# Slots of one SBUF ring padded from 8,224 to 8,448 bytes

## The chip, the cores and the metric

The kernel runs on one core of a Trainium2 chip. The metric is the device time in microseconds; the kernel before was timed three times, with a median of 2720.2 us (2720.13 to 2723.26). One more execution was taken with the hardware profiler; all rows below are from that one. Engines: PE is TensorE's matmul, PEld its weight load, DVE VectorE, ACT ScalarE, POOL GpSimd, SP the engine that issues the DMAs.

## The reference

One encoder block over 2,048 positions of width 1,024, in float32:

```python
mod = silu(c) @ w_ada + b_ada                       # shift, scale, gate, twice
h = rms_norm(x, norm1_g) * (1 + scale1) + shift1
q, k, v, xr, gr = split(h @ w_in)                   # 5 x 512 columns
attn = dilated_mixture_attention(q, k, v, positions)    # 8 heads, 3 dilations
rec = bidirectional_rg_lru(xr, gr, ...)             # conv, gates, two scans, gelu gate
mixed = concat([rms_norm(attn, attn_out_g), rms_norm(rec, lru_out_g)])
x = x + gate1 * (mixed @ w_out)
h2 = rms_norm(x, norm2_g) * (1 + scale2) + shift2
x = x + gate2 * (square(relu(h2 @ w_ff1)) @ w_ff2)  # 1024 -> 4096 -> 1024
return rms_norm(x, final_g)
```

## The kernel before

**Matmuls.** Every large product is made of float32r matmuls in which both operands are split into a rounded high half and a remainder (`halves`, `wsplit`): high x high, high x low, low x high, three matmuls for one. Nearly all go through `mm` (L89). The second argument of `mm` is the operand that is loaded as weights (128 columns of 4 bytes, so 512 bytes of each partition); the third is the one that moves through the array (mostly 512 columns, so 2,048 bytes of each partition). In a row of the trace such a matmul reads `pmm<-moving,weights`: `pmm`, `pg` and `ptr` are the three rings of PSUM banks.

**Stages, in order of time.** The six modulation vectors (`ada`) and the projections by `w_in` (to about 660 us; weights in `wh`, activations in `hT`; the recurrence runs beside them), attention (to about 1,217 us), `w_out` (`wout_tile`, to about 1,360 us), the first feed-forward matrix (FFN1, to about 2,050 us) and the second (FFN2, to the end). Both feed-forward products use a seven-product scheme over 2 x 2 blocks (`LEFT`, `RIGHT`). In FFN1 a step of the loop over `steps1` is 12 matmuls; its weights, split by `w1_prep`, lie in three tiles of tag `L8` (`new_slots`), and what moves is `hT`, `wh` or, for one product, two further `L8` tiles. In FFN2 a step of `steps2` is 24 matmuls; its weights are the hidden blocks, which `prep2` writes into a new `L8` tile at each step (ACT rounds at L1508, POOL subtracts at L1510), and what moves is `wf`. There are 7 x 16 = 112 such steps; the first 96 are those of the products that come before the last one in `ORD2`. During the last product DVE also finishes the rows of the output (`finals`).

**Rings.** A tile is taken from a ring of slots by its tag (`sbt`, with the number of slots in `BUFS`): `L8` has 6 slots, `st` 6, `hT` 8, `wh` 4, `r4` 4, `t2` 8, `bc` 2, `wf` 4, `xr` 4, `C` 16. A ring's slot is as large as the largest tile of its tag. Most tiles of `L8` have 8,192 bytes in each partition; four, the `xrn` tiles, have `S + 8` = 2,056 numbers, 8,224 bytes. So the six `L8` slots lie 8,224 bytes apart. `L8` and `st` come first in their memory; all other rings lie behind `L8`. In the built program the slots begin at these places:

| ring | start of its slots, bytes past a multiple of 256 | past a multiple of 512 |
|---|---|---|
| `L8`, slots 0 to 5 | 0, 32, 64, 96, 128, 160 | 0, 32, 64, 96, 128, 160 |
| `st`, `t2`, `bc`, `hT`, `r4`, `wh`, `wf`, `xr`, `w2`, `C`, `xt`, `row` | 192 | 192 |

The other slots' sizes are multiples of 512. The weights of a matmul begin a multiple of 512 bytes into their slot in all of the 512-column matmuls spoken of below. FFN1's three weight tiles lie in slots 0, 3 and 5; FFN2's step goes through all six slots in turn (in the trace's stretch from 2184.68 us: slots 1, 5, 4, 3, 0, 2).

```python
xrn = [sbt("L8", (P, S + 8)) for j in range(4)]                       # L470
w, (hi, lo) = wslot[(s + 4) % 6], bks[m]                              # FFN1, a step
for l, r in ((w[:, 0, ks], hi[:, k]), (w[:, 0, ks], lo[:, k]), (w[:, 1, ks], hi[:, k])):
    mm(pt, l, r, n == 0, n == 11)
mm(pts[i], h[:, 0, ts], w[:, 0], p == 0, False)                       # FFN2, 8 tiles of a step
mm(pts[i], h[:, 0, ts], w[:, 1], False, False)
mm(pts[i], h[:, 1, ts], w[:, 0], False, p == NP - 1)
```

The order of the work is that of the program: every engine takes its instructions as they are written, and all DMAs are issued by SP.

Of the kernel before, what the change touches and what calls it, by code (L numbers as in the profile page):

```python
# [17 lines left out]
P = 128  # L18
S = 2048
# [37 lines left out]
def block_kernel(ctx: ExitStack, tc, x, vecs, pos, w_ada, b_ada, fg, w_in, lwa, lwx, w_out, w1, w2, cst, out):  # L57
# [13 lines left out]
    def sbt(tag, shape, dt=F32):  # L71
        cnt[0] += 1
        return (sx if tag in ("L8", "st") else sb[0]).tile(list(shape), dt, tag=tag, name=f"{tag}_{cnt[0]}", bufs=BUFS[tag])
# [393 lines left out]
    for t in xs:  # L467
        norm_x(t)
    SY.dma_start(Done, onr)
    xrn = [sbt("L8", (P, S + 8)) for j in range(4)]  # L470
    for j in range(4):
        G.memset(xrn[j][:, 0:2], 0.0)
        G.memset(xrn[j][:, S + 2:S + 8], 0.0)
# [1174 lines left out]
```

## Time and profile before

| what | value |
|---|---|
| median of three runs | 2720.2 us (2720.13 to 2723.26) |
| the profiled execution: its own time, its span | 2720.57 us, 2718.7 us |
| mean granted TensorE clock | 0.949 |
| PE, PEld busy | 94%, 76% of the span |
| DVE, POOL, ACT busy | 61%, 44%, 40% |
| DMA engines busy (main queue) | 55.4% |

A busy PE in this table is not a PE at its peak: matmuls overlap, and their ends are modelled. What one matmul takes from the next is read from their starts: so many in so many microseconds.

### The profile page before, as it was taken

Reading aid. Unit: us, or ns where it says so; the run is one execution under the profiler, and the core shown is the slowest. Engines: PE = TensorE matmul, PEld = TensorE weight load, DVE = VectorE, ACT = ScalarE, POOL = GpSimd, SP = SyncE. Lnnn points to the kernel's source line nnn. Section 1 sums busy time; section 2 is a strip of 40 time slices with the busy share of each in tenths; the row PEclk is TensorE's granted clock in tenths of the full one; section 3 lists DMA queues with packets and bytes.
Section 4 is the critical chain, followed back from the end, with each engine's and each line's share of the span. In section 5 each row is a group of like instructions: output and inputs, shape, how many; then the busy total and the mean of one; then the engine's idle time right before and its main releaser. Section 6 shows DMA issues by size and latency. Waiting matters only on the chain.

```text
span 2718.7 us, 32852 instructions
## 1 busy us (share of the span) xinstructions
PE 2542.2 (94%) x11321; PEld 2075.0 (76%) x11321; DVE 1656.9 (61%) x2963; ACT 1093.5 (40%) x1701; POOL 1200.8 (44%) x914
## 2 busy tenths in 40 slices
PE   4998988999999999999879999899998999999996
PEld 3776767778888888887757877688886888888885
DVE  6588777974444444436767657977774224312688
ACT  2243675571122222222455445655553323232223
POOL 2343444642012211131357667766556445544544
PEclk9998989998898888899989999999998999999998
DMA  6765356566544455547766666644437465536554
GB/s 266 266 225 186 96 178 211 203 163 159 122 109 118 117 132 140 125 141 235 243 202 214 204 195 209 209 152 155 140 129 276 164 209 187 170 121 210 191 201 176
DMA packets 267491, 486.01 MB, mean 179 GB/s; under 512 B 88874, under 2 KB 122406, under 8 KB 259754
## 3 DMA queue, kind: packets, MB, share of 16 engines
q1 hardware_dynamic: 267324, 483.92, 55.4%
q8 instruction: 89, 1.46, 0.2%
q14 instruction: 78, 0.64, 0.1%
HBM read 330.45 MB, written 153.19 MB: 178 GB/s over the span
## 4 chain that ended last, share of the span: by engine, by line
PE 36%; POOL 6%; DVE 5%; DMA 5%; issue 3%; ACT 1%; SPq 0%; POOLq 0%; DVEq 0%; ACTq 0%
PE pmm L89 15%; PE pg L89 13%; PE ptr L89 8%; POOL st L1218 3%; DMA st<-Dh 3%; POOL ry L301 1%; DVE L L1223 1%; POOL t L1380 1%; DMA Dhc<-st 1%; POOL L L1510 0%; DVE C L1545 0%; DVE C L1549 0%; DVE L L1200 0%; POOL L L1381 0%; DMA r<-in_w 0%
## 5 line engine op out<-in xcount | busy, mean ns | idle before, releaser
L1510 POOL TENSOR_TENSOR L<-xr,L 128x512 fp32r<-128x512 f32 x224 | 317.5, 1438 | 285.9 <-ACT L L1508 278.7
L89 PE MATMUL pmm<-hT,wh 128*128 128x512 f32 x1536 | 376.1, 401 | 5.9 <-POOL hT L341 3.3
L89 PEld LDWEIGHTS pmm<-hT,wh 128*128 128x128 f32 x1536 | 293.6, 193 | 78.3 <-POOL hT L341 7.7
L89 PE MATMUL pmm<-wf,L 128*128 128x512 f32 x1008 | 292.4, 398 | 17.8 <-ACT L L1508 12.8
L89 PE MATMUL pg<-wf,L 128*128 128x512 f32 x1008 | 290.0, 396 | 0.0
L858 DVE CUSTOM_DVE_ANT_0 junk<-ptr,mb 128x256 bf16<-128x256 f32 (+2 forms) x384 | 140.1, 365 | 174.3 <-PE ptr L89 157.3
L89 PEld LDWEIGHTS pmm<-wf,L 128*128 128x128 f32 x1008 | 190.5, 189 | 65.2 <-ACT L L1508 13.2
L912 ACT ACTIVATE t<-pmm 128x512 f32<-128x512 f32 x160 | 94.8, 596 | 353.5 <-PE pmm L89 352.3
L1223 DVE TENSOR_TENSOR L<-st,L 128x512 fp32r<-128x512 f32 x167 | 191.4, 1151 | 63.3 <-ACT L L1222 62.0
L89 PEld LDWEIGHTS pg<-wf,L 128*128 128x128 f32 x1008 | 190.7, 189 | 45.2
L257 POOL TENSOR_TENSOR wh<-r,wh 128x512 fp32r<-128x512 f32 x88 | 139.8, 1610 | 173.5 <-DVE wh L95 106.1
L301 POOL TENSOR_TENSOR ry<-rv,mhalf 128x1 f32<-128x1 f32 x80 | 51.5, 645 | 350.4 <-DVE rv L299 341.3
L89 PE MATMUL ptr<-wf,L 128*128 128x512 f32 x672 | 193.9, 397 | 0.0
L1218 POOL TENSOR_TENSOR st<-r,r 128x512 f32<-128x512 f32 x96 | 135.9, 1423 | 109.3 <-DVE L L1223 94.7
L89 PE MATMUL pmm<-hT,hT 66*128 66x256 f32 (+5 forms) x672 | 177.1, 399 | 0.0
L1223 DVE TENSOR_TENSOR wf<-st,wf 128x512 fp32r<-128x512 f32 x80 | 59.8, 747 | 190.6 <-ACT wf L1222 190.6
L1222 ACT ACTIVATE L<-st 128x512 fp32r<-128x512 f32 x168 | 105.5, 628 | 163.6 <-POOL st L1218 84.9
L89 PE MATMUL ptr<-hT,hT 128*128 128x256 f32 (+5 forms) x672 | 163.6, 390 | 4.1 <-DVE mc L858 4.0
L1222 ACT ACTIVATE wf<-st 128x512 fp32r<-128x512 f32 x80 | 50.4, 631 | 281.7 <-PE pg L89 216.5
L89 PE MATMUL pg<-t,L 128*66 128x192 f32 (+2 forms) x756 | 159.0, 348 | 1.8 <-POOL L L1051 1.8
L89 PE MATMUL pmm<-hT,L 128*128 128x512 f32 x576 | 149.7, 408 | 10.0 <-ACT L L1222 7.1
L89 PEld LDWEIGHTS pmm<-hT,hT 128*128 128x128 f32 (+1 forms) x672 | 148.8, 278 | 9.1 <-issue 2.6
(326 smaller groups left out, 5276.3 us busy)
## 6 DMA issues: line engine op xcount, KB each, us to landing
xr<-Dhx SPq DMA_DIRECT2D x112, 512.0 KB
w<-in_w SPq DMA_DIRECT2D x192, 256.0 KB
r<-in_w SPq DMA_DIRECT2D x64, 512.0 KB
Dhx<-t SPq DMA_DIRECT2D x128, 256.0 KB
L<-in_w_ada SPq DMA_DIRECT2D x24, 1024.0 KB
r<-in_w_in SPq DMA_DIRECT2D x40, 512.0 KB
st<-Dh SPq DMA_DIRECT2D x72, 256.0 KB
r<-in_x SPq DMA_DIRECT2D x26, 512.0 KB
```

What stands on the lines that cost most here:

```text
L89: T.matmul(o, l, r, start=st, stop=sp, skip_group_check=True)
L257: G.tensor_tensor(w[:, 1, cs], raw[:, cs], f(w[:, 0, cs]), ALU.subtract)
L301: G.tensor_tensor(y, v_, mhalf[:, 0:1], ALU.pow)
L858: V.tensor_tensor_reduce(junk[:, 0:nk], p_[:, e, 0:nk], mb1[:, off:off + nk], 1.0, -3e38, ALU.add, ALU.max, mc[:, idx:idx + 1])
L912: A.activation(pf, pS, AF.Exp)
L1218: eng.tensor_tensor(o, a, b, ALU.add if sign > 0 else ALU.subtract)
L1222: A.activation(hi, raw, AF.Copy)
L1223: lo_eng.tensor_tensor(lo, raw, f(hi), ALU.subtract)
L1380: G.tensor_tensor(x6, x6, h, ALU.subtract)
L1510: G.tensor_tensor(h[:, 1, e], r_[:, e], f(h[:, 0, e]), ALU.subtract)
```

## The change

```diff
@@ -467,7 +467,7 @@
     for t in xs:
         norm_x(t)
     SY.dma_start(Done, onr)
-    xrn = [sbt("L8", (P, S + 8)) for j in range(4)]
+    xrn = [sbt("L8", (P, S + 64))[:, 0:S + 8] for j in range(4)]
     for j in range(4):
         G.memset(xrn[j][:, 0:2], 0.0)
         G.memset(xrn[j][:, S + 2:S + 8], 0.0)
```

The four `xrn` tiles are taken with 2,112 numbers and used as before with 2,056. The ring's slots become 8,448 bytes, and everything behind `L8` moves up by 6 x 224 = 1,344 bytes. Every engine has the same instructions in the same order with the same waits; the places in DRAM are the same. What differs is where operands lie in SBUF:

| ring | bytes past a multiple of 256, after | past a multiple of 512, after |
|---|---|---|
| `L8`, slots 0 to 5 | 0, 0, 0, 0, 0, 0 | 0, 256, 0, 256, 0, 256 |
| the others of the table above | 0 | 0 |

## Rows read from the trace of the kernel before

**Rows 1.** The page's first part: busy time, share, instructions of each engine.

```profile
PE 2542.2 (94%) x11321; PEld 2075.0 (76%) x11321; DVE 1656.9 (61%) x2963; ACT 1093.5 (40%) x1701; POOL 1200.8 (44%) x914
```

**Rows 2.** The page's fourth part: chain that ended last, by engine.

```profile
PE 36%; POOL 6%; DVE 5%; DMA 5%; issue 3%; ACT 1%; SPq 0%; POOLq 0%; DVEq 0%; ACTq 0%
```

**Rows 3.** Two windows: us, busy of each engine (instructions), clock, DMA share, GB/s.

```profile
2080.00:2600.00 520.00, 520.00 (x2239) 420.53 (x2238) 185.61 (x236) 163.01 (x214) 266.63 (x193) 1.00 0.54 187
1760.00:2040.00 280.00, 280.00 (x1204) 225.77 (x1203) 211.79 (x245) 161.31 (x273) 171.59 (x114) 1.00 0.41 146
```

**Rows 4.** The chain of waits from 1,599 us: start, length, what.

```profile
1599.93 5.43 DMA st<-Dh
...
1645.46 2.60 PE ptr L89 x10
...
1703.96 0.72 PE ptr L89 x3
...
1757.48 3.75 PE pg L89 x12
...
2032.37 2.80 PE pg L89 x12
...
2046.37 2.81 PE pmm L89 x12
...
2597.02 0.71 PE pg L89 x3
...
2599.11 0.60 DVE C L1532
```

**Rows 5.** PE timeline, moving and weights both at 192; last row: weights in `L8`.

```profile
95.67 20.11 PE L89 MATMUL pmm<-hT,wh 128*128 128x512 f32 x88
...
1217.85 11.15 PE L89 MATMUL pmm<-wh,r 128*128 128x512 f32 x48
...
1229.21 11.39 PE L89 MATMUL pmm<-wh,L 128*128 128x512 f32 x48
```

**Rows 6.** PE timeline in FFN2: the first row of seven successive steps.

```profile
2184.68 0.85 PE L89 MATMUL pmm<-wf,L 128*128 128x512 f32 x3
...
2190.29 0.86 PE L89 MATMUL pmm<-wf,L 128*128 128x512 f32 x3
...
2195.89 0.85 PE L89 MATMUL pmm<-wf,L 128*128 128x512 f32 x3
...
2201.39 0.86 PE L89 MATMUL pmm<-wf,L 128*128 128x512 f32 x3
...
2206.98 0.86 PE L89 MATMUL pmm<-wf,L 128*128 128x512 f32 x3
...
2212.58 0.87 PE L89 MATMUL pmm<-wf,L 128*128 128x512 f32 x3
...
2218.16 0.85 PE L89 MATMUL pmm<-wf,L 128*128 128x512 f32 x3
```

**Rows 7.** PE timeline in the recurrence: moving in `L8`, weights in `bc`.

```profile
287.07 1.56 PE L89 MATMUL pg<-L,bc 128*128 128x512 f32 x6
288.47 5.62 PE L89 MATMUL pmm<-hT,wh 128*128 128x512 f32 x24
```

**Rows 8.** Groups of 512-column matmuls with weights outside `L8`.

```profile
L89 PE MATMUL pmm<-hT,wh 128*128 128x512 f32 x1536 | 376.1, 401 | 5.9 <-POOL hT L341 3.3 <-DVE hT L340 1.1 <-DVE hT L341 1.0
L89 PE MATMUL pmm<-hT,r 128*128 128x512 f32 x384 | 100.6, 415 | 2.2 <-DVE L L1200 2.2
L89 PE MATMUL pmm<-wh,hT 128*128 128x512 f32 x384 | 96.0, 405 | 6.8 <-DVE st L411 6.8
```

**Rows 9.** DMA queue, 6.5-9, 9-11.5, 100.3-102.8 us: packets, MB, share of 16 engines.

```profile
q1 hardware_dynamic: 273, 1.05, 102.6%
...
q1 hardware_dynamic: 269, 1.04, 102.6%
...
q1 hardware_dynamic: 245, 0.95, 93.1%
```

## The prediction

> **What bounds the kernel now.** I read the busy time first: PE is at it for 94% of the span and no other engine for more than 61% [rows 1]. The average says little, so the next view is the chain of waits. Of its shares, PE has by far the largest, POOL, DVE and DMA 5 to 6% each [rows 2]. In order of time the chain has three kinds of stretch [rows 4]. Up to 1645 us, in the first part of FFN1, it runs through loads of `st` from `Dh`, POOL sums and evictions: PE is fed late there, and a faster PE would wait longer. From 1645.46 to 1704.68 us and from 1757.48 to 2049.18 us it is PE alone, one group of 12 matmuls behind the other. FFN2 is PE alone too, until its last product begins at about 2597 us and DVE's work on the output rows takes over. The two windows show the same from the other side: PE is busy for all of 520 and all of 280 us at granted clock 1.00, while DVE, ACT and POOL leave 24% and more free [rows 3].
>
> **What a matmul costs there, and on what that depends.** The change adds, removes and moves no instruction. It can act only through the places of operands in SBUF, so I looked for rows in which the same operation has operands in different places, and counted from start to start.
>
> Weights and moving operand both 192 bytes past a multiple of 256: 88 projections in a row span 20.11 us. A single one is modelled as 401 ns long on average [rows 8], overlapping the next, so from the first start to the last it is (20.11 - 0.40) us / 87 = 226.6 ns from one to the next [rows 5].
>
> Weights in `L8`, moving operand at 192: in `wout_tile`, the same lines with the weights in `r4` take (11.15 - 0.40) us / 47 = 228.7 ns, and 11 us later with the weights in `L8` (11.39 - 0.40) us / 47 = 233.8 ns [rows 5]. In FFN2, step after step of 24 matmuls with the same code and only another slot, the differences of the starts give 5.61, 5.60, 5.50, 5.59, 5.60, 5.58 us for slots 1, 5, 4, 3, 0, 2 [rows 6]: 233.8, 233.3, 229.2, 232.9, 233.3, 232.5 ns, on average 33.48 us / 144 = 232.5 ns. In FFN1, 2.80 us / 12 = 233.3 ns [rows 4].
>
> Moving operand in `L8`, weights in `bc` at 192: (288.47 - 287.07) us / 6 = 233.3 ns [rows 7].
>
> So a 512-column matmul costs 226.6 ns (228.7 in the shorter row) where both operands have the same remainder by 256 (and here by 512), and 229 to 234 ns where they differ, whichever of the two lies in `L8`. Slot 4, with its 229.2 ns, is only 64 bytes off. I read this as a cost of the difference of the two places. After the change that difference is 0 by 256 everywhere, and by 512 in slots 0, 2 and 4; in slots 1, 3 and 5 it is 256. No 512-column matmul of this trace has a difference of 256. Its cost is bounded by the rows from 226.6 ns (nothing lost) to 233.8 ns (the dearest row at full clock with weights in `L8`). I take 226.6, since every row fits a pattern that repeats every 256 bytes, but one that repeats every 512 fits nearly as well; both ends stay in the range.
>
> A rule speaks against any effect. The Trainium skill ("SBUF — State Buffer", section "Who interferes with whom") gives TensorE two independent SBUF read ports, one for the moving operand and one for the weights, and says that TensorE never waits on anyone. By that the sum would be 0 and the time 2720.6 us. The trace differs: 5.50 against 5.61 us for the same step, by slot alone [rows 6].
>
> **The sum.** It is made against the profiled execution, 2720.57 us (span 2718.7), 0.4 us above the median of 2720.2.
> - FFN2 up to the last product: 96 steps x 24 = 2,304 matmuls x (232.5 - 226.6 = 5.9 ns) = 13.6 us. All on the path: the chain is PE to 2597 us, and what follows on DVE starts from PE's evictions [rows 4].
> - FFN1 from 1757.48 to 2049.18 us: 291.7 / 0.2333 = 1,250 matmuls x 6.7 ns (233.3 - 226.6) = 8.4 us, on the path.
> - FFN1 from 1645.46 to 1704.68 us: 254 x 6.7 ns = 1.7 us, on the path; the feeders' stretch behind it starts from a PE row.
> - FFN1 otherwise: of its 224 steps x 12 = 2,688 matmuls 1,184 are left, most of them before 1645 us. They get shorter too, but the chain is the loads' and POOL's there; I count nothing. If the feeders were bound to PE after all it would be 1,184 x 6.7 ns = 7.9 us.
> - The two `w_out` tiles from `L8`: 48 x 7.2 ns = 0.3 us. The recurrence: 192 matmuls (4 column blocks, 2 x 2 gates, 4 stretches, 3 each) like those of rows 7 x 6.7 ns = 1.3 us; whether they are on the path the chain does not show, I take half, 0.6.
> - The last 16 steps of FFN2: DVE's chain; nothing.
> - VectorE, ScalarE, POOL and DMAs: nothing on the path. With 24% free on DVE in the tighter window [rows 3], feeding a PE that is 2.8% faster fits.
>
> Together 13.6 + 8.4 + 1.7 + 0.3 + 0.6 = 24.6 us: 2696 us. With the uncounted 7.9 us gained it would be 2688; with a quarter lost to feeders that come late, 2702.
>
> **The rivals.**
> 1. *The pattern repeats every 512 bytes.* Then slots 0, 2 and 4 gain and 1, 3, 5 do not. FFN2: (6.7 + 5.9 + 2.6) ns / 6 x 2,304 = 5.8 us; FFN1, whose weights lie in slots 0, 3 and 5: a third of 1,504 x 6.7 ns = 3.4 us; the rest 0.3. That is 9.5 us: 2711 us; if the odd slots rise from 233.3 to 233.8 ns, 1.1 us less, 2712. For it: the cheap rows are all equal by 512 too. Against it: nothing but the shorter pattern's being simpler.
> 2. *Not the difference, but the place itself: weights are cheap at 192 and dear at 0.* Slower. The two rings on which the projections rest would move from the good place to that of slot 0. The first three groups of rows 8 are 1,536 + 384 + 384 = 2,304 matmuls, x 6.7 ns = 15.4 us, and FFN2 would go from 232.5 to slot 0's 233.3 ns, 1.8 us. With two thirds of the first on the path: 2720.6 + 10.3 + 1.8 = 2733 us. It decides once a matmul with both operands at 0 costs more than the 232.5 ns that FFN2's cost now: then nothing is gained in FFN2 and the projections lose. For it: in rows 6 the cost falls as the slot nears 192. Against it: rows 7, where the weights do lie at 192 and the matmul still costs 233.3 ns.
> 3. *No change.* The 233 ns belong to the stages (other engines reading and writing beside), not to the places. 2720.6 us. For it: most weights in `L8` are used in FFN1 and FFN2. Against it: rows 6, one stage, and the two rows of `w_out`.
> 4. *Only the DMAs gain.* Rings behind `L8` are now reached at multiples of 256. The packets of 4,096 bytes take, as 16 engines x share x window / packets, 150.3 ns into slot 4 (+128), 152.6 into slot 3 (+96), 152.0 into `r4` (+192) [rows 9]: no order by place, and at most 1.5% between them. If 1.5% of the chain's DMA (5% of 2718.7 = 136 us [rows 2]) went away, that is 2.0 us: 2718.6 us. The Trainium skill ("DMA: Bandwidth & Descriptors", section "How a descriptor splits into AXI transactions") has a descriptor that does not start at a multiple of 256 bytes fetch from the boundary below it; 2,048 bytes at +192 would then take 70 beats instead of 64, and an estimate by that page is 136 x 6 / 70 = 11.7 us. Rows 9 don't bear it out: by it +96 would be the cheapest of the three, and it is the dearest.
>
> **How the numbers follow.** My forecast 0.52; rival 1, 0.28; rival 2, 0.08; rival 3 and rival 4 together 0.12, both of them no change by the bound of about 0.2% (5.4 us) that a measurement of this kernel can tell. The predicted time is 2696 us. Its own range is 2688 to 2702; with rival 1 the range is 2688 to 2714, which holds 0.8. Faster: 0.52 + 0.28 and a little of the rest, 0.81; same 0.11; slower 0.08.
>
> **What would show it.** Right: FFN2's steps take 24 x 226.6 ns = 5.44 us whatever the slot, and a window of 40 us in FFN1 or FFN2 holds 176 matmuls in place of 172; the `w_out` tiles from `L8` cost what those from `r4` do; FFN1 before 1645 us takes as long as before; projections stay at 226.6 ns. Rival 1: steps alternate between 5.44 and about 5.6 us. Rival 2: the projections' 88 matmuls take 20.5 us and more in place of 19.7. Wrong altogether: steps of 5.50 to 5.61 us again, in the same order; or short steps with PE waiting for ACT, POOL or DVE between them, and a span that has not moved.

## The result and the profile after

The changed kernel takes 2701.5 us (median of six runs, 2698.0 to 2702.6) against 2721.2 us (2720.1 to 2724.5) for the kernel before in the same comparison: a ratio of 0.9923, with a 95% interval of 0.991 to 0.9936. The forecast was 2696 us, with a range of 2688 to 2714. Of the 24.6 us that the sum promised, 19.7 came. The profiled execution took 2699.56 us, 21.0 us less than that of before.

First the page's busy times, which answer to [rows 1]. PE's is 34.1 us less; those of the other engines differ by about half a per cent or less. The totals do not say in which stage, or whether on the path.

```profile
PE 2508.1 (93%) x11321; PEld 2068.0 (77%) x11321; DVE 1665.2 (62%) x2963; ACT 1093.6 (41%) x1701; POOL 1205.5 (45%) x914
```

Next two windows of the kernel after (us, busy time and instructions of PE, PEld, DVE, ACT and POOL in this order, granted clock, DMA share, GB/s). The first lies in FFN2, the second is the stretch of FFN1 in [rows 3].

```profile
2080.00:2560.00 480.00, 480.00 (x2119) 397.45 (x2118) 172.86 (x221) 153.93 (x202) 251.43 (x182) 1.00 0.56 189
1760.00:2040.00 280.00, 280.00 (x1233) 231.74 (x1232) 214.55 (x248) 163.97 (x277) 170.50 (x114) 1.00 0.40 146
```

PE is busy all the time in both, as before, at the same granted clock. What has changed is the count: 1,233 matmuls in 280 us in place of 1,204, so 227.1 ns in place of 232.6; in FFN2, 480 us / 2,119 = 226.5 ns in place of 232.2.

The PE timeline of the kernel after (start, length, line, operation, operands). First the two pairs of `w_out` tiles, which answer to the lower rows of [rows 5]; then a projection and the recurrence, as in [rows 7]; then the first rows of seven successive steps of FFN2, as in [rows 6].

```profile
1220.69 11.15 PE L89 MATMUL pmm<-wh,r 128*128 128x512 f32 x48
1232.04 11.19 PE L89 MATMUL pmm<-wh,L 128*128 128x512 f32 x48
```

```profile
94.81 20.56 PE L89 MATMUL pmm<-hT,wh 128*128 128x512 f32 x90
...
289.92 1.52 PE L89 MATMUL pg<-L,bc 128*128 128x512 f32 x6
291.28 5.60 PE L89 MATMUL pmm<-hT,wh 128*128 128x512 f32 x24
```

```profile
2179.98 0.84 PE L89 MATMUL pmm<-wf,L 128*128 128x512 f32 x3
...
2185.42 0.84 PE L89 MATMUL pmm<-wf,L 128*128 128x512 f32 x3
...
2190.86 0.84 PE L89 MATMUL pmm<-wf,L 128*128 128x512 f32 x3
...
2196.30 0.84 PE L89 MATMUL pmm<-wf,L 128*128 128x512 f32 x3
...
2201.74 0.84 PE L89 MATMUL pmm<-wf,L 128*128 128x512 f32 x3
...
2207.18 0.84 PE L89 MATMUL pmm<-wf,L 128*128 128x512 f32 x3
...
2212.62 0.84 PE L89 MATMUL pmm<-wf,L 128*128 128x512 f32 x3
```

With the weights in `r4` nothing has moved (11.15 us for 48, before and after). With the weights in `L8` the 48 take 11.19 in place of 11.39 us. The projections are where they were: (20.56 - 0.40) us / 89 = 226.5 ns. The recurrence's six take 1.36 us, 226.7 ns each, in place of 1.40. In FFN2 the starts lie 5.44 us apart six times in a row, whatever the slot: 226.7 ns for each of 24 matmuls. The slots in odd places, 256 bytes off by 512, cost the same as the even ones.

The chain of waits after (start, length, what), beside [rows 4]:

```profile
1562.32 4.67 DMA st<-Dh
...
1645.25 2.56 PE ptr L89 x10
...
1707.65 2.73 PE pg L89 x12
...
1757.16 4.86 PE pg L89 x12
...
2034.05 2.72 PE pg L89 x12
...
2044.96 0.70 DVE t L1375
...
2059.47 0.80 PE pmm L89
...
2589.50 0.68 PE pg L89 x3
```

The same places in the kernel before, of which [rows 4] did not show these two:

```profile
2051.97 0.70 DVE t L1375
...
2066.05 0.79 PE pmm L89
```

Read from top to bottom, this is where the time came from. At 1645 us the two kernels are level (0.2 us apart), though they were not so before: at `w_out` the kernel after was 2.8 us behind (1220.69 against 1217.85 us). From 1645 us PE gains up to 0.08 us with each group of 12, and has lost nearly all of it again by 1757 us (0.3 us apart). At the end of FFN1 the kernel after is 7.0 us ahead, at the start of FFN2 6.6, and it ends 21 us ahead. The last PE row of each chain is the place where the chain leaves PE, and not the same matmul in both: FFN2's last product begins at 2603.05 us before and at 2582.54 after, 20.5 us apart.

### The profile page after: what moved, and what is told of

Same layout as the page of the kernel before. It is cut to its first block, busy times and chain, and to the rows that moved or that the text cites. A ratio compares the mean times of both kernels' runs of the same rounds, so it can differ in the third digit from the quotient of the medians.

```text
span 2697.6 us, 32852 instructions
## 1 busy us (share of the span) xinstructions
PE 2508.1 (93%) x11321; PEld 2068.0 (77%) x11321; DVE 1665.2 (62%) x2963; ACT 1093.6 (41%) x1701; POOL 1205.5 (45%) x914
## 4 chain that ended last, share of the span: by engine, by line
PE 36%; POOL 6%; DMA 5%; DVE 5%; issue 3%; ACT 1%; SPq 0%; POOLq 0%; DVEq 0%; ACTq 0%
PE pmm L89 15%; PE pg L89 13%; PE ptr L89 8%; POOL st L1218 3%; DMA st<-Dh 3%; POOL ry L301 1%; DMA Dhc<-st 1%; POOL L L1510 1%; DVE L L1223 0%; POOL t L1380 0%; DVE C L1549 0%; DVE L L1200 0%; DVE C L1559 0%; DMA r<-in_w 0%; PE ptr L322 0%
## 5 line engine op out<-in xcount | busy, mean ns | idle before, releaser
L1510 POOL TENSOR_TENSOR L<-xr,L 128x512 fp32r<-128x512 f32 x224 | 323.8, 1467 | 269.6 <-ACT L L1508 266.2
L89 PE MATMUL pmm<-wf,L 128*128 128x512 f32 x1008 | 285.9, 391 | 20.1 <-ACT L L1508 13.2
L89 PE MATMUL pg<-wf,L 128*128 128x512 f32 x1008 | 284.1, 390 | 0.0
L89 PEld LDWEIGHTS pmm<-wf,L 128*128 128x128 f32 x1008 | 189.6, 188 | 62.3 <-ACT L L1508 13.6
```

The lines of the kernel that those rows point to most:

```text
L89: T.matmul(o, l, r, start=st, stop=sp, skip_group_check=True)
L1510: G.tensor_tensor(h[:, 1, e], r_[:, e], f(h[:, 0, e]), ALU.subtract)
```

## Experiments

Theory: the cost of a 512-column matmul hangs on the difference of the places of its two operands, by 256 bytes. Rival A: operands must begin at multiples of 256 bytes. Rival B: it is the `L8` ring that has to. Rival C: the gains of FFN1 and FFN2 are not separate, or late feeding hides one of them. All kernels are the changed one with a pad of some bytes in one place; instructions and waits are the same. The four below were timed five times or more each, together with the kernel before, whose 23 runs have a median of 2721.9 us (2716.6 to 2729.3).

**All rings at +192.**

```diff
+    pad = sx.tile([P, 48], F32, tag="pad", name="pad", bufs=1)
     onr = sbt("L8", (2, S))
```

> The changed kernel with 192 bytes put in front of the `L8` ring: every slot of every ring lies 192 bytes past a multiple of 256, none at a multiple of 256. Theory (the cost hangs on the difference of the two operands' places by 256): the difference is 0 everywhere, so FFN2's steps take 5.44 us, FFN1's groups of 12 take 2.72 us, and the time is that of the changed kernel, 2701 us (2697 to 2705). Rival (operands have to begin at multiples of 256 bytes): weights and moving operands are off by 192 alike, the matmuls of FFN1, FFN2 and the projections take 233 ns, and the time is 2721 us or more.

Measured: 2697.8 us (2696.3 to 2705.0), ratio 0.9912 (0.9897 to 0.9928). The windows of 1800 to 2000 us and of 2100 to 2500 us in this kernel:

```profile
1800.00:2000.00 200.00, 200.00 (x885) 165.64 (x884) 156.30 (x181) 118.76 (x201) 127.95 (x87) 1.00 0.44 156
2100.00:2500.00 400.00, 400.00 (x1766) 331.31 (x1766) 120.43 (x167) 128.34 (x171) 201.71 (x149) 1.00 0.54 183
```

The same windows of the kernel before, then of the changed one:

```profile
1800.00:2000.00 200.00, 200.00 (x860) 161.27 (x859) 150.07 (x174) 116.33 (x196) 124.22 (x83) 1.00 0.43 151
2100.00:2500.00 400.00, 400.00 (x1722) 323.44 (x1722) 115.63 (x158) 126.87 (x168) 195.59 (x146) 1.00 0.52 178
```

```profile
1800.00:2000.00 200.00, 200.00 (x884) 165.62 (x883) 153.96 (x178) 119.04 (x202) 126.84 (x85) 1.00 0.42 152
2100.00:2500.00 400.00, 400.00 (x1766) 331.24 (x1765) 122.54 (x172) 128.48 (x171) 198.62 (x148) 1.00 0.53 180
```

400 us / 1,766 = 226.5 ns in FFN2, as in the changed kernel, though no slot begins at a multiple of 256 any more. Rival A falls.

**`L8` at 0, everything else at +192.**

```diff
     onr = sbt("L8", (2, S))
+    pad = sx.tile([P, 48], F32, tag="pad", name="pad", bufs=1)
```

> The changed kernel with 192 bytes put behind the `L8` ring: all six `L8` slots at multiples of 256, all other rings at +192, as they were before. Theory (difference): every matmul with one operand in `L8` is what slot 0's was before, 233.3 ns; FFN2's steps take 5.60 us in all six slots, FFN1's groups 2.80 us; 2701.5 + 2304 x 6.7 ns (15.4) + 7 = 2724 us (2719 to 2728). Rival (what helps is that `L8` itself begins at multiples of 256): steps of 5.44 us and 2701 us.

Measured: 2723.1 us (2718.1 to 2726.7, 12 runs), ratio 1.0001 (0.9991 to 1.0011). The same windows:

```profile
1800.00:2000.00 200.00, 200.00 (x861) 160.85 (x861) 150.16 (x175) 116.00 (x196) 123.59 (x84) 1.00 0.43 151
2100.00:2500.00 400.00, 400.00 (x1716) 322.26 (x1715) 116.46 (x157) 125.54 (x167) 196.94 (x146) 1.00 0.52 177
```

Padded slots, all of them at multiples of 256, and the whole gain is gone: 400 us / 1,716 = 233.1 ns, what slot 0 cost before [rows 6]. Rival B falls.

**Only FFN1 and the recurrence apart** (the pad in front of `t2`, `bc`, `hT`, `r4`, `wh`):

```diff
+    pad = sb[0].tile([P, 48], F32, tag="pad", name="pad", bufs=1)
     vr = sbt("t2", (P, P))
```

> The changed kernel with 192 bytes put in front of the rings that live until the end of FFN1 (`t2`, `bc`, `hT`, `r4`, `wh` at +192; `L8`, `st` and FFN2's rings at 0). Theory: FFN1 and the recurrence pay the difference again, FFN2 does not: FFN1's groups of 12 take 2.80 us, FFN2's steps 5.44 us, and the 7 us that FFN1's end had moved forward in the changed kernel are given back: 2708 us (2705 to 2713). Rival (the gain of the two stages is not separate, FFN1's part is lost to late feeding anyway): 2701 us.

Measured: 2707.3 us (2705.3 to 2710.4), ratio 0.9945 (0.9931 to 0.9958).

```profile
1800.00:2000.00 200.00, 200.00 (x861) 160.85 (x860) 149.59 (x174) 116.23 (x196) 123.19 (x84) 1.00 0.42 150
2100.00:2500.00 400.00, 400.00 (x1766) 331.31 (x1766) 119.40 (x163) 129.84 (x172) 201.31 (x150) 1.00 0.54 185
```

**Only FFN2 apart** (the pad in front of `wf`):

```diff
+    pad = sb[0].tile([P, 48], F32, tag="pad", name="pad", bufs=1)
     for s in range(P2):
         prep2(s)
```

> The changed kernel with 192 bytes put in front of FFN2's ring `wf` (`wf`, `C`, `xt` at +192, all else at 0). Theory: FFN2's steps take 5.60 us as in slot 0 before, FFN1's groups 2.72 us; 2701.5 + 2304 x 6.7 ns = 2717 us (2714 to 2720). Rival (DVE's and the DMAs' end of FFN2 hides part of it): 2710 us or less.

Measured: 2717.2 us (2709.9 to 2725.4, 12 runs), ratio 0.9982 (0.997 to 0.9995).

```profile
1800.00:2000.00 200.00, 200.00 (x884) 165.62 (x883) 156.33 (x181) 118.58 (x201) 127.90 (x87) 1.00 0.43 156
2100.00:2500.00 400.00, 400.00 (x1716) 322.29 (x1715) 115.35 (x158) 126.18 (x167) 193.93 (x145) 1.00 0.52 176
```

In each of the two, one window has the fast count and the other the slow one. Against the changed kernel's 2701.5 us, FFN1 apart costs 5.8 us and FFN2 apart 15.7; together 21.5, and both apart at once cost 21.6 (2723.1). These are differences of medians, and the twelve executions with FFN2 apart lie up to 15 us apart, so they add up within some microseconds. The profiled executions say it more sharply. The table gives the time from the start of one matmul to the start of another, the same two in each kernel (us, one profiled execution of each):

| stretch | before | changed | all at +192 | FFN2 apart | FFN1 apart | `L8` at 0, rest +192 |
|---|---|---|---|---|---|---|
| FFN1, first part (to the group at 1645 us) | 281.3 | 279.1 | 280.1 | 281.4 | 279.9 | 280.8 |
| from there to the group at 1757 us | 111.8 | 111.7 | 112.7 | 111.8 | 111.2 | 111.0 |
| from there to FFN1's last matmul | 294.3 | 287.6 | 286.4 | 286.4 | 294.4 | 294.4 |
| FFN2, 96 steps | 538.4 | 524.4 | 525.7 | 540.9 | 524.6 | 540.9 |
| FFN2, last product | 97.3 | 96.7 | 96.8 | 98.1 | 96.8 | 96.9 |

The late stretch of FFN1 is short in the three kernels in which FFN1's operands have the same remainder, FFN2 in the three in which FFN2's have it. So rival C falls. Measured against the gap everywhere, FFN2's steps bring about three quarters of the gain and FFN1 one quarter; measured against the kernel before, in which some slots cost less, FFN2's 96 steps bring 13.9 of 21.0 us.

**Other differences, one run each.** The pad behind `L8` with 32, 64, 128 and 224 bytes, so that weights in `L8` lie so much below the moving operand by 256:

```diff
     onr = sbt("L8", (2, S))
+    pad = sx.tile([P, 8], F32, tag="pad", name="pad", bufs=1)     # 8, 16, 32, 56
```

> The changed kernel with 32 bytes behind the `L8` ring: `L8` 32 bytes below the other rings by 256, in all six slots. Theory (the difference alone sets the cost): as slot 5 before (160 against 192), FFN2's steps 5.60 us. Rival (slot 5 was dear because it lies off a multiple of 64; here only the others do): some other value, the same for all slots.

> The changed kernel with 64 bytes behind the `L8` ring: `L8` 64 below the others. Theory (the difference alone): as slot 4 before (128 against 192), FFN2's steps 5.50 us in all slots, 2704 us for FFN2's part and some 2706 us in all. Rival (the cost grows or not with the place itself): 5.60 us.

> The changed kernel with 128 bytes behind the `L8` ring: the difference is 128 by 256. Theory: as slot 2 before (64 against 192), FFN2's steps 5.58 us. Rival (the pattern repeats every 128 bytes, and 256 is more than is needed): 5.44 us and 2701 us.

> The changed kernel with 224 bytes behind the `L8` ring: `L8` 32 above the others by 256, a difference that FFN2 has not had. Theory (no difference but 0 is free): 5.5 to 5.65 us a step. Rival (only weights below the moving operand are dear): 5.44 us.

The window of 2100 to 2500 us in each, in this order:

```profile
2100.00:2500.00 400.00, 400.00 (x1716) 321.34 (x1715) 116.53 (x157) 127.35 (x169) 197.11 (x146) 1.00 0.52 176
```

```profile
2100.00:2500.00 400.00, 400.00 (x1749) 328.19 (x1748) 116.93 (x164) 128.32 (x170) 201.03 (x147) 1.00 0.53 180
```

```profile
2100.00:2500.00 400.00, 400.00 (x1723) 324.34 (x1722) 116.34 (x159) 126.20 (x169) 196.89 (x146) 1.00 0.52 178
```

```profile
2100.00:2500.00 400.00, 400.00 (x1716) 321.99 (x1716) 117.72 (x157) 128.06 (x169) 199.15 (x148) 1.00 0.52 174
```

Per matmul that is 233.1, 228.7, 232.2 and 233.1 ns; per step of 24 it is 5.59, 5.49, 5.57 and 5.59 us. The first three are what slots 5, 4 and 2 cost before (5.60, 5.50, 5.58 us [rows 6]), although here the six slots together have that cost. So what slot 4 had was neither its number nor its place, but its difference. 128 is not enough: the pattern does not repeat there. Of the differences tried, only 0 and 256 are free. The single times are 2726.8, 2707.0, 2722.3 and 2731.4 us, beside one run of the kernel before at 2715.8; single runs of one kernel lay up to 15 us apart above, and the counts carry the argument, not these times.

## Why the prediction was right

**The mechanism: right and shown.** Both halves of it were tested by themselves: it is the difference (+192 for all is fast, a gap of 192 is slow), and it repeats by 256 and not by 512 (even and odd slots both 5.44 us). The value taken for the one unknown, 226.6 ns for a difference of 256, was measured at 226.7. That it was taken so was a judgement: no row of before tells a period of 256 from one of 512, and with the latter the sum came to 2711 us. Rival 1, repetition by 512, would have shown steps that alternate. Rival 2, the place itself, falls with the projections, which moved from 192 to 0 and stayed at 226.5 ns. (What I wrote for it, that the cost falls as the slot nears 192, is not in [rows 6]: slot 5, the nearest, takes 5.60 us.) Rival 3 falls with FFN1 apart and FFN2 apart: the same stage is fast or slow by a pad alone.

The terms below are those of the two profiled executions. With the 0.2 us by which the kernel after led at 1645 us they make up the 21.0.

**FFN2: 13.6 us expected, 13.9 came.** The 96 steps took 524.4 us in place of 538.4. Of that 13.2 us lie in the last 95 of them, 5.8 ns for each matmul, and 0.8 in the first, which runs partly on the lower level of the clock in both (granted 0.66 from 2064 to 2073 us before, 0.78 from 2058 to 2067 after); with all rings at +192 that first step is no shorter than before, so the 0.8 us is not shown to belong to the change. FFN2's load of `xr` cost 0.4 us in front of it. The last product, which I had counted at nothing, brought 0.5 us (20.5 ahead at its start, 21.0 at the end). Two readings of mine were a little off and change nothing here: the chain leaves PE at 2597.73 us, one step before the last product begins at 2603.05, and a window of 40 us held 173 or 174 matmuls before, not 172.

**Late FFN1: 8.4 us expected, 6.7 came** (0.3 us ahead at 1757 us, 7.0 at the end). I had taken 233.3 ns from one group of 2.80 us for all. The mean group of before is 2.796 us, since one group in seven (both operands in `L8`) takes 2.76 to 2.78; after it is 2.72. So the 104 groups behind the first got 0.075 us shorter each, 7.8 us. Of that, 1.1 us went in the first group, which took 4.86 in place of 3.75 us. The windows of 1750 to 1765 us, before and then after, show the granted clock (the number behind POOL's) at 0.89 and 0.77. PE had stood idle for about 4 of these 15 us in both, and the stretch on the lower of the two levels lasted longer. This loss is not the change's as such: the two kernels with all rings at +192 and with FFN2 apart, whose FFN1 matmuls have the same cost, gained 7.9 us in this stretch.

```profile
1750.00:1765.00 15.00, 11.04 (x40) 8.42 (x40) 15.00 (x16) 9.71 (x17) 15.00 (x10) 0.89 0.48 163
```

```profile
1750.00:1765.00 15.00, 11.17 (x36) 8.67 (x37) 15.00 (x16) 8.74 (x16) 15.00 (x10) 0.77 0.47 163
```

**FFN1 from 1645 to 1704 us: 1.7 expected, 0.1 kept.** This step failed. PE did gain 1.6 us there, but I let the gain pass because the feeders' stretch behind it begins at a PE row of the chain. From about 1711 us the chain is DVE's, ACT's and POOL's work and loads, 45.7 us long in both kernels (from the DVE row of `L8` at 1711.81 before and 1711.45 after to the `pg` group at 1757.48 and 1757.16). PE arrives there 1.8 us ahead and waits longer. It is the same in the other two kernels with a faster FFN1: for the whole stretch from 1645 to 1757 us they take 112.7 and 111.8 us, and the kernel before 111.8. A chain names who was last, not who would have been last a microsecond earlier.

**FFN1 before 1645 us: nothing expected, nothing shown.** In the kernel after this part is 2.2 us shorter. But with all rings at +192 it is 1.2 us shorter and with FFN2 apart not at all, and with FFN1 apart, where its matmuls are as dear as before, 1.4 us. So the cost of the matmuls does not show in it, which bears out that others set the pace there; the 7.9 us of the forecast's upper end did not come.

**The recurrence and `w_out`: 0.9 expected, not seen at FFN1.** Both got shorter by about what was forecast (11.19 for 11.39 us, 1.36 for 1.40), but the kernel after reached FFN1 2.0 us later. Most of that was lost early: in the windows of 200 to 265 us, before and then after, the granted clock is 0.89 and 0.84, and PE gets through 211 and 200 matmuls. The kernel with `L8` at 0 and the rest at +192, which gains nothing, loses as much there: its clock in this window is 0.84 with 198 matmuls, and the recurrence's row of [rows 7] starts at 289.87 us in it, at 289.92 in the changed kernel and at 287.07 before. So the loss does not come from cheaper matmuls; why the executions differ there was not traced. Of `w_out`'s own rows, the 228.7 ns of the shorter row is no cost of the places: its first matmul takes 313 ns to the next and the nine behind it about 231, and the rest 226 to 227.

```profile
200.00:265.00 65.00, 58.02 (x211) 41.68 (x211) 58.24 (x81) 24.16 (x37) 23.26 (x15) 0.89 0.61 204
```

```profile
200.00:265.00 65.00, 58.05 (x200) 40.51 (x199) 55.35 (x77) 21.29 (x34) 21.00 (x13) 0.84 0.59 199
```

**The DMAs: rival 4 had no part in it that can be seen.** With all rings at +192 no slot that a transfer reaches begins at a multiple of 256, and the gain is all there (2697.8 us). The median packet takes the same time before, after and with all rings at +192: 84 ns for 2,048 bytes, 159 for 4,096 and 311 for 8,224. The 11.7 us of the estimate are nowhere to be found.

## What to carry to other kernels

Where PE runs without a gap, read its cost per matmul from starts, in windows of equal clock, and compare the same line with operands in different buffers: 5.50 against 5.60 us for the same step was the sign, before anything was changed. For float32r matmuls like these (128 x 128 weights, 512 columns), keep the weights and the moving operand at the same remainder by 256 bytes; a slot that is 32 bytes too long moves the ring's own slots, and all rings behind it, against each other. Whether other types and shapes of matmul gain by it, no run here shows. Count a faster PE only where the chain is PE's own, and not where it begins a stretch in which others are waited for.

## What the runs showed of the hardware

The cost of a 512-column float32r matmul at granted clock 1.00, by how far its weights begin above the moving operand, by 256 bytes:

| difference | ns per matmul | from |
|---|---|---|
| 0, and 256 by 512 | 226.5 to 226.7 | after, all at +192 |
| -64 | 228.7 | gap of 64 |
| 128 | 232.2 | gap of 128 |
| -32 | 233.1 | gap of 32 |
| +64 (-192) | 233.1 | gap of 192 |
| +32 (-224) | 233.1 | gap of 224 |

I had not expected that it is so exact (every step of FFN2 5.44 us), that 64 below is cheap and 64 above is dear, or that a loss of 3% can come from nothing but two addresses. The Trainium skill ("SBUF — State Buffer", section "Who interferes with whom") has TensorE's two read ports independent and TensorE waiting for no one. By that the places should not matter; here they do, by up to 6.6 ns a matmul. Why the difference matters, and what the two streams may share, no run here shows.
